# A hybrid encoder layer on one core: loads of the reverse attention a step ahead, operand splits inside the last steps of an epoch, the first row tile of the output projection between the last norms

## The chip, the core and the metric

The kernel runs on one NeuronCore of a Trainium2 chip. The metric is the device time of one execution in microseconds (us). Before the change three runs took 3528.44, 3544.09 and 3544.74 us, median 3544.09. The profiled execution took 3531.64 us and its span is 3529.9 us.

## The reference

One layer of a bidirectional encoder for 2048 tokens of width 1024, all in float32: two mixers side by side (a RWKV-7 recurrence and a gated linear attention, GLA, each run forward and backward over the sequence), an output projection, a gated FFN and a gate over per-layer embeddings.

```
xn = rms_norm(h, norm_mix_pre);  z = xn @ w_in
y_rwkv = rwkv7_mixer(z_rwkv)     # S = S*w + (S@-kk) b + v k, forward and reverse; group norm; gate
y_gla  = gla_mixer(z_gla)        # chunks of 64, forward and reverse, summed; rms_norm * silu(g)
h = h + rms_norm(concat(y_rwkv, y_gla) @ w_out, norm_mix_post)
hn = rms_norm(h, norm_ffn_pre)
f  = (silu(hn @ ffn_gate) * (hn @ ffn_up)) @ ffn_down
h = h + rms_norm(f, norm_ffn_post)
gate = sigmoid(h @ ple_gate + ple_gate_b)
h = h + rms_norm(gate * (p @ ple_proj), norm_ple)
```

## The kernel before

Three phases follow one another. The input phase (to about 1030 us) makes the projections and the forward half of GLA. The recurrence, `phase_b`, handles RWKV in 8 units of 16 steps; each step is a handful of short matmuls, and the loop also pops two lists of side work: `fill`, the reverse half of GLA (`gla_tail`: 17 items, popped on the odd steps under 12 of a unit, which the trace has between 1140 and 1391 us), and `todo`, the group norms and gates of the RWKV output, one per step. The last norms have no steps left to lie beside: they are popped in a loop of their own once the steps are done, at about 1770 to 1796 us. A norm sums and squares on VectorE (DVE) and ScalarE (ACT), takes a power on GpSimd (POOL), writes and reads the scratch `d_yn`, and is turned by TensorE (PE) into the bank `pty` before DVE multiplies it with the gate and it is stored to `d_y`.

`phase_c` begins when these are stored. It takes 16 row tiles of the output projection (`out_tile`, t = 0 to 15). A float32 product is made of three passes in fp32r: both operands are split into a high part (a cast on ACT, line 1056) and the rest (a subtraction on DVE, line 1057), and `mm3` (lines 73 to 75) adds high x high, low x high and high x low. A tile is 8 slices x 2 column halves x 3 = 48 matmuls of 128x512. Then come six epochs E0 to E5 of steps: FFN gate and up for each half of the tokens (E0, E1: 22 steps each), the FFN's down product in three parts (E2 to E4: 8 steps each) and the embedding gate (E5: 8 steps). A step multiplies by a scheme of seven products in place of eight, in the order B11, T2, B21, T3, T1, T4, B22, each of 3n matmuls (n is 3 in E2, 4 elsewhere). The moving operand of the seven products is fixed for an epoch and stays in SBUF, split; `moving` loads and splits the seven at each change of epoch, after the last step's products in the program. Each operand of n=4 is two loads (`rawm`), two casts and two subtractions of 128x1024.

All loads and stores are issued by SyncE (SP), in order. Every engine runs its instructions in one fixed order; a scheduler has set that order beforehand by the times of a simulated run, so program text that moves can change the order on all five engines. PSUM banks of the products: `pA` (pool psA), `pB`, `pC`, two each; `pt` is for transposes and for the scratch `jk` of the row norms.

Of the kernel before, what the change touches and what calls it, by code (L numbers as in the profile page):

```python
# [631 lines left out]
def phase_b(ctx, ctr, tc, k):  # L632
# [316 lines left out]
    for n in range(len(steps) + LAG):  # L949
# [35 lines left out]
    while todo:  # L985
        todo.pop(0)()


def gla_tail(k, yp, ip, ps):
# [6 lines left out]
    def step(q, h):  # L996
# [6 lines left out]
        nc.sync.dma_start(sg, k.d["sg"][128 * h:128 * h + 128, q * TQ:q * TQ + TQ])  # L1003
        po = ps.tile([128, 4, 128], F32, tag="psg", name="po")
# [27 lines left out]
    lag = []  # L1032

    def run(q, h):
        if q is not None:
            lag.append(step(q, h))
# [4 lines left out]
    return [(lambda a: lambda: run(*a))(a) for a in seq]  # L1041
# [22 lines left out]
def out_weights(ctx, tc, k):  # L1064
# [12 lines left out]
    return wo  # L1077

# [7 lines left out]
def phase_c(ctx, tc, k, wo):  # L1086
# [36 lines left out]
    def moving(e, src, r0, n, ops=OPS):  # L1123

        for o in ops:
            pool = w if o in OPS[:4] else sl
            mv[o] = []
            for b in range(0, n, 2):
                m = min(2, n - b)
                raw = cp.tile([128, 2, 512], F32, tag="t", name="rawm")[:, :m]  # L1130
                if o[0] == "B":
                    r, c = r0 + n * (o[1] == "2") + b, 512 * (o[2] == "2")
                    nc.sync.dma_start(raw, src[r:r + m, :, c:c + 512].rearrange("j p f -> p j f"))
                else:
                    nc.sync.dma_start(raw, k.d["mt"][e, int(o[1]) - 1, :, b:b + m])
                hl = [pool.tile([128, 2, 512], F32R, tag=f"{o}{b // 2}{t}", bufs=1, name=f"{o}{t}")[:, :m] for t in "hl"]
                split_into(nc, *hl, raw)
                mv[o].append(hl)
# [41 lines left out]
    def products(st, n, t):  # L1180

        def prod(bank, p, o, first):
            sh, s_l = st[p]
            if first and k.bias and bank is not B:
                k.bias(bank, int(bank is C))
                first = False
            for j in range(n):
                mm3(nc, bank, sh[:, j], s_l[:, j], mv[o][j // 2][0][:, j % 2], mv[o][j // 2][1][:, j % 2], first and j == 0, j == n - 1, skip_group_check=True)
# [5 lines left out]
        prod(A, 1, "B11", True)  # L1194
        p1 = u("p1")
# [3 lines left out]
        V.tensor_add(u2, B, p1)  # L1199
        prod(A, 2, "B21", False)  # L1200
        prod(B, 7, "T3", False)
        u3 = u("u3")
        V.tensor_add(u3, B, p1)
        while late and late[0][0] <= t:
            late.pop(0)[1]()
        prod(C, 5, "T1", True)
        c = [cp.tile([128, D], F32, tag="t", name="c") for _ in range(2)]
        V.tensor_add(c[1][:, 512:], C, u3)
        prod(B, 4, "T4", False)
        V.tensor_add(c[1][:, :512], B, p1)  # L1210
        prod(C, 3, "B22", False)
# [50 lines left out]
    def out_split(raw, m):  # L1262
        hl = []
        for g in range(2):
            hl.append([sp.tile([128, 4, 128], F32R, tag="s" + x, name="s" + x) for x in "hl"])
            split_into(nc, *hl[g], raw[:, 4 * g:4 * g + 4, 128 - 128 * m:256 - 128 * m])
        return hl

    def out_tile(t, i, hl):
        x = xtile(rows("x", i))  # L1270
        A = psA.tile([128, 512], F32, tag="pA", name="pA")
        B = psB.tile([128, 512], F32, tag="pB", name="pB")
        for c, bank in enumerate((A, B)):
            for j in range(KT):
                mm3(nc, bank, *[v[:, j % 4] for v in hl[j // 4]], *[v[:, j % 2] for v in wo[c][j]], j == 0, j == KT - 1)
            if c == 0:
                while late and late[0][0] <= t:
                    late.pop(0)[1]()
        r = root([A, B])
# [9 lines left out]
        late.append((t + 2, lambda: transposed(x, k.d["hT"][p // 4, :, :, q:q + 128].rearrange("k p t -> p k t"), True)))  # L1289

    def out_projection():
        raws = [out_operand(0), out_operand(1)]
        hl = out_split(raws[0], 0)
        e = E[0]
        for t in range(16):
            p, m = t // 2, t % 2
            nx = out_split(raws[(t + 1) // 2], 1 - m) if t < 15 else prepare(0)
            out_tile(t, PAIRS[p][m], hl)
# [5 lines left out]
            if t == 14:  # L1304
                flush()
                moving(0, e.src, e.r0, e.n, OPS[4:])
            hl = nx
        moving(0, e.src, e.r0, e.n, OPS[:4])
# [68 lines left out]
    def pre_ple(c_):  # L1377
        return [xtile(rows("e", PAIRS[c_][m])) for m in range(2)]

    def post_ple(c_, x, A, c):  # L1380
        S.activation(c[0][:, :512], A, AF.Sigmoid)
        res = [xtile(rows("h2", PAIRS[c_][m])) for m in range(2)] if c_ == 7 else x
# [55 lines left out]
    for t, (e, i) in enumerate(steps):  # L1438
# [10 lines left out]
        A, c = products(st, ep.n, 16 + t)  # L1449
# [4 lines left out]
        if i + 1 == len(ep.parts) and e + 1 < len(E):  # L1454
            nxt = E[e + 1]
            moving(e + 1, nxt.src, nxt.r0, nxt.n)
# [78 lines left out]
def body(tc, k):  # L1535
    with ExitStack() as ctx:
# [23 lines left out]
        next(b, None)  # L1560
# [18 lines left out]
```

## Time and profile before

| | before |
|---|---|
| runs, us | 3528.44, 3544.09, 3544.74 (median 3544.09) |
| profiled execution / span, us | 3531.64 / 3529.9 |
| TensorE busy | 3322.2 us (94%) |
| VectorE / ScalarE / GpSimd busy | 2607.5 (74%) / 1705.3 (48%) / 450.5 us (13%) |
| mean granted TensorE clock | 0.962 |
| HBM moved | 403.18 MB read, 211.81 MB written |

TensorE is busy nearly all the time, so what can be gained is in two places: the gaps in which it waits, and the stretches in which its granted clock is at the lower of its two levels and the same matmul takes up to twice as long. A row of a window view gives, for each engine, the busy us and instructions in a stretch, then PEclk (the mean granted clock, 1.00 is full) and the share of DMA time. A row of a timeline gives the start, the length, the engine, the line, what is written from what, and in brackets the idle time before it and what ended it.

### The profile page before, as it was taken

The numbers are of one execution on the slowest core, as the hardware profiler recorded it, in microseconds if no ns is written. First come the engines' busy times: TensorE is split into PE (matmuls) and PEld (weight loads), VectorE is DVE, ScalarE is ACT, GpSimd is POOL, SyncE is SP. The second block draws the span as 40 slices with busy tenths as digits, with TensorE's granted clock in tenths as the row PEclk, the third lists the DMA queues.
The fourth block names the chain that finished last, engine by engine and source line by source line (L and its number), as shares of the span: only waits on it lengthen the run. The fifth ranks groups of instructions, "written<-read, shape, count | busy, mean of one in ns | idle before, by whom it ended". The sixth has DMA issues, their size and how long they took to land.

```text
span 3529.9 us, 57042 instructions
## 1 busy us (share of the span) xinstructions
PE 3322.2 (94%) x20880; PEld 2839.5 (80%) x20880; DVE 2607.5 (74%) x4481; ACT 1705.3 (48%) x3547; POOL 450.5 (13%) x898
## 2 busy tenths in 40 slices
PE   7989999989998999999879899999999999999998
PEld 6979988878976888888758688887888878778776
DVE  6998898887895667678644667777666566778887
ACT  5665566655555546665624532334332333334454
POOL 2000000000002445556111100000000000001112
PEclk9999999989998879999989999999999999999999
DMA  7766655646664445463355845556222243666775
GB/s 249 248 237 195 188 198 193 213 138 219 202 199 148 132 134 161 112 182 87 114 177 188 289 143 179 191 192 225 84 86 82 84 134 132 227 203 245 278 258 185
DMA packets 390436, 629.25 MB, mean 178 GB/s; under 512 B 122790, under 2 KB 223142, under 8 KB 390156
## 3 DMA queue, kind: packets, MB, share of 16 engines
q1 hardware_dynamic: 390156, 625.61, 53.6%
q8 instruction: 165, 2.70, 0.3%
q14 instruction: 115, 0.94, 0.1%
HBM read 403.18 MB, written 211.81 MB: 174 GB/s over the span
## 4 chain that ended last, share of the span: by engine, by line
PE 73%; DVE 12%; DMA 7%; ACT 4%; issue 3%; SPq 1%; POOL 0%; DVEq 0%; ACTq 0%; POOLq 0%
PE pB L73 7%; PE pB L75 6%; PE pB L74 6%; PE pA L74 5%; PE pA L75 5%; PE pA L73 5%; PE pC L74 4%; PE pC L75 4%; PE pC L73 4%; PE pz L73 3%; PE pz L75 3%; PE pz L74 3%; PE pg L673 3%; PE ph L792 3%; PE pf L809 2%
## 5 line engine op out<-in xcount | busy, mean ns | idle before, releaser
L1056 ACT CAST sh<-raws 128x512 fp32r<-128x512 f32 (+1 forms) x456 | 277.6, 610 | 672.8 <-PE pB L74 357.4
L73 PE MATMUL pz<-xh,wh 128*128 128x256 f32 (+1 forms) x1728 | 501.0, 291 | 13.3 <-DMA wh<-d_ws 7.1
L75 PE MATMUL pz<-xh,wl 128*128 128x258 f32 (+1 forms) x1728 | 495.9, 290 | 5.6 <-DVE wl L218 3.1
L74 PE MATMUL pz<-xl,wh 128*128 128x256 f32 (+1 forms) x1728 | 496.5, 288 | 0.2 <-DVE xl L271 0.2
L1057 DVE TENSOR_TENSOR sl<-raws,sh 128x512 fp32r<-128x512 f32 (+1 forms) x456 | 306.0, 672 | 115.8 <-ACT sh L1056 110.6
L73 PEld LDWEIGHTS pz<-xh,wh 128*128 128x128 f32 x1728 | 330.9, 192 | 22.6 <-issue 13.7
L75 PEld LDWEIGHTS pz<-xh,wl 128*128 128x128 f32 x1728 | 328.2, 191 | 15.9 <-issue 6.8
L74 PEld LDWEIGHTS pz<-xl,wh 128*128 128x128 f32 x1728 | 331.5, 192 | 6.3 <-issue 5.3
L1221 POOL TENSOR_TENSOR st<-st 128x1 f32<-128x1 f32 x64 | 17.4, 271 | 1630.4 <-ACT jk L1220 1629.9
L792 PE MATMUL ph<-x,wpi 128*128 128x128 f32 x1024 | 174.6, 300 | 11.4 <-ACT wpi L788 10.0
L73 PE MATMUL pA<-B11h,sh 128*128 128x512 f32 x360 | 147.9, 412 | 22.1 <-ACT B11h L1056 18.5
L809 PE MATMUL pf<-sv,Ht 128*128 128x64 f32 x1024 | 156.7, 283 | 10.2 <-ACT sv L814 5.8
L792 PEld LDWEIGHTS ph<-x,wpi 128*128 128x128 f32 x1024 | 142.3, 203 | 22.1 <-ACT wpi L788 16.2
L809 PEld LDWEIGHTS pf<-sv,Ht 128*128 128x128 f32 x1024 | 140.3, 201 | 22.5 <-ACT sv L814 9.4
L74 PE MATMUL pA<-B11l,sh 128*128 128x512 f32 x360 | 148.1, 411 | 4.1 <-DVE B11l L1057 4.1
L75 PE MATMUL pA<-B11h,sl 128*128 128x512 f32 x360 | 146.9, 408 | 0.0
L673 PE MATMUL pg<-ar,bk 64*128 64x128 f32 x1024 | 141.1, 295 | 5.0 <-DVE x L676 3.2
L73 PE MATMUL pB<-T3h,sh 128*128 128x512 f32 x360 | 143.4, 398 | 0.0
L75 PE MATMUL pB<-T3h,sl 128*128 128x512 f32 x360 | 143.0, 397 | 0.0
L74 PE MATMUL pB<-T3l,sh 128*128 128x512 f32 x360 | 142.5, 396 | 0.0
L1056 ACT CAST sh<-s 128x512 fp32r<-128x512 f32 (+1 forms) x76 | 46.3, 609 | 186.6 <-PE pA L74 164.0
L673 PEld LDWEIGHTS pg<-ar,bk 64*128 64x128 f32 x1024 | 119.4, 196 | 19.5 <-DVE x L676 4.2
(637 smaller groups left out, 8983.4 us busy)
## 6 DMA issues: line engine op xcount, KB each, us to landing
wh<-d_ws SPq DMA_DIRECT2D x81, 512.0 KB, 3.8
wl<-d_ws SPq DMA_DIRECT2D x81, 512.0 KB, 5.0
d_mt<-rawt SPq DMA_DIRECT2D x92, 256.0 KB, 2.5
raws<-in_ffn_gate SPq DMA_DIRECT2D x44, 512.0 KB, 4.9
raws<-in_ffn_up SPq DMA_DIRECT2D x44, 512.0 KB, 4.1
rawm<-d_mt SPq DMA_DIRECT2D x44, 512.0 KB, 8.7
d_hid<-c SPq DMA_DIRECT2D x88, 256.0 KB, 2.8
d_ar<-st SPq DMA_DIRECT2D x32, 512.0 KB, 3.7
```

The source lines that it names most:

```text
L73: nc.tensor.matmul(out, ah, bh, start=start, stop=False, **kw)
L74: nc.tensor.matmul(out, ah, bl, start=False, stop=False, **kw)
L75: nc.tensor.matmul(out, al, bh, start=False, stop=stop, **kw)
L673: nc.tensor.matmul(pg[h][:, j], bk[HR[h], j], ar[HR[h], j], start=True, stop=True)
L792: nc.tensor.matmul(ph[:, h, j], w[:, h, j], x[:, j0 + j, 4 * h:4 * h + 2, :], start=True, stop=True)
L809: nc.tensor.matmul(pf[:, h, j0 + j], H[:, h, j], SV[p, d, c][:, h, j0 + j], start=True, stop=True)
L1056: nc.scalar.copy(hi, src)
L1057: nc.vector.tensor_sub(lo, src, hi.bitcast(F32))
L1221: G.tensor_add(st[:, 2:3], st[:, 0:1], st[:, 1:2])
```

## The change

1. `gla_tail`: the loads of an item (`fetch`) are an item of their own, before the item that computes (`step`). The list is 34 long and popped on every step under 12; while it lasts, `todo` is popped on odd steps only.
2. `phase_b` yields before and after each of the norms that are left at its end. Between two of them `body` loads the 128 tokens of the first row tile of the output projection (512 KB), splits them, and runs that tile's two x 24 matmuls into two `pA` banks. Tiles from t = 1 on use the banks in another order.
3. The transposes of the last two row tiles are put off by a step.
4. `moving` is a generator. In the last step of an epoch (and in tile 15) it is resumed before the products and after the first six of them: each time one operand is loaded and the one before is split; what is left follows after the products.
5. In the last step of E5 the residual tiles are loaded before the products.

```diff
-            if s % 2 == 1 and s < 12 and fill:
+            if s < 12 and fill:
                 fill.pop(0)()
-            if todo:
+            if todo and (s % 2 or s >= 12 or not fill):
                 todo.pop(0)()
...
+    yield
     while todo:
         todo.pop(0)()
+        yield
...
+        return qi, o, sg
+
+    def step(q, h, qi, o, sg):
         po = ps.tile([128, 4, 128], F32, tag="psg", name="po")
...
+    def ahead(q, h):
+        if q is not None:
+            ready.append(fetch(q, h))
...
+    return [(lambda f, a: lambda: f(*a))(f, a) for a in seq for f in (ahead, run)]
...
+def out_products(k, hl, bank, wo):
+    for j in range(KT):
+        mm3(k.nc, bank, *[v[:, j % 4] for v in hl[j // 4]], *[v[:, j % 2] for v in wo[j]], j == 0, j == KT - 1)
...
+    def settle(o, raws):
+
+        pool = w if o in OPS[:4] else sl
+        mv[o] = []
+        for b, raw in enumerate(raws):
+            hl = [pool.tile([128, 2, 512], F32R, tag=f"{o}{b}{t}", bufs=1, name=f"{o}{t}")[:, :raw.shape[1]] for t in "hl"]
+            split_into(nc, *hl, raw)
+            mv[o].append(hl)
+
+    def moving(e, ops):
+
+        fetched = []
         for o in ops:
...
+            fetched.append((o, fetch(e, o)))
+            yield
+            if len(fetched) > 1:
+                settle(*fetched.pop(0))
+        while fetched:
+            yield
+            settle(*fetched.pop(0))
...
-    def products(st, n, t):
+    def products(st, n, t, change):
...
         prod(A, 1, "B11", True)
+        next(change, None)
         p1 = u("p1")
...
-        late.append((t + 2, lambda: transposed(x, k.d["hT"][p // 4, :, :, q:q + 128].rearrange("k p t -> p k t"), True)))
+        late.append((t + 2 + (t > 13), lambda: transposed(x, k.d["hT"][p // 4, :, :, q:q + 128].rearrange("k p t -> p k t"), True)))
...
-        A, c = products(st, ep.n, 16 + t)
+        last = i + 1 == len(ep.parts) and e + 1 < len(E)
+        change = moving(e + 1, OPS) if last else iter(())
+        next(change, None)
+        A, c = products(st, ep.n, 16 + t, change)
...
-        next(b, None)
+        next(b)
+        with ExitStack() as ef:
...
+            hl = out_split(k, fp, raw)
+            banks = [k.psA.tile([128, 512], F32, tag="pA", name="pA") for _ in range(2)]
+            for c in range(2):
+                out_products(k, hl, banks[c], mv[c])
+                next(b, None)
+        k.first = banks
+        for _ in b:
+            pass
         bl.close()
         phase_c(ctx, tc, k, mv)
```

How the order of instructions moves, at the three places that matter most. TensorE at the end of the recurrence, before; `pf` and `ph` are of the last steps, `pty` are the turned group norms, `B11h` is the first slice of the output weights and `sh` of a row tile:

```order
L869 MATMUL pty<-ident,yn 128x128 x4
L809 MATMUL pf<-sv,Ht 128x64 x4
L869 MATMUL pty<-ident,yn 128x128 x4
L809 MATMUL pf<-sv,Ht 128x64 x2
L869 MATMUL pty<-ident,yn 128x128 x16
L73 MATMUL pA<-B11h,sh 128x512
L74 MATMUL pA<-B11l,sh 128x512
L73 MATMUL pB<-B21h,sh 128x512
```

The same place after the change; the 48 matmuls into `pA` lie between the last `pf` and the last sixteen `pty`, of which the first and last ones are shown:

```order
L809 MATMUL pf<-sv,Ht 128x64 x2
L869 MATMUL pty<-ident,yn 128x128 x4
L809 MATMUL pf<-sv,Ht 128x64 x2
L73 MATMUL pA<-B11h,sh 128x512
L74 MATMUL pA<-B11l,sh 128x512
...
L74 MATMUL pA<-T3l,sh 128x512
L75 MATMUL pA<-T3h,sl 128x512
L869 MATMUL pty<-ident,yn 128x128 x16
L73 MATMUL pB<-B11h,sh 128x512
L74 MATMUL pB<-B11l,sh 128x512
```

Before, the sixteen `pty` of the last two norms stood in front of the first row tile; now they stand behind all of it and in front of the second.

VectorE at the change from E0 to E1, before; `c<-pC` and `c<-pB` empty the last step's banks, `sl` and `raws` belong to the next step's stationary operand, `B11l` and `T2l` are the next epoch's splits:

```order
L1203 TENSOR_TENSOR u_25790<-pB,p_25750 128x512
L1115 TENSOR_TENSOR rawt<-rawt 128x512
L1057 TENSOR_TENSOR sl<-s_25698,sh 128x512
L1208 TENSOR_TENSOR c<-pC,u_25790 128x512
...
L1210 TENSOR_TENSOR c<-pB,p_25750 128x512
...
L1212 TENSOR_TENSOR c<-pC,u_25764 128x512
...
L1057 TENSOR_TENSOR B11l<-rawm,B11h 128x1024 x2
L1057 TENSOR_TENSOR T2l<-rawm,T2h 128x1024 x2
```

The same place after the change:

```order
L1247 TENSOR_TENSOR u_25828<-pB,p_25764 128x512
L1137 TENSOR_TENSOR rawt<-rawt 128x512
L1066 TENSOR_TENSOR sl<-s_25704,sh 128x512
L1066 TENSOR_TENSOR B11l<-rawm,B11h 128x1024
...
L1066 TENSOR_TENSOR B11l<-rawm,B11h 128x1024
L1066 TENSOR_TENSOR T2l<-rawm,T2h 128x1024
...
L1066 TENSOR_TENSOR T2l<-rawm,T2h 128x1024
L1066 TENSOR_TENSOR B21l<-rawm,B21h 128x1024
...
L1253 TENSOR_TENSOR c<-pC,u_25828 128x512
L1256 TENSOR_TENSOR c<-pB,p_25764 128x512
```

Five splits of 128x1024 now stand ahead of the two instructions that empty `pC` and `pB`; they stood behind them.

SyncE at the same change, before; `rawt` are loads for later operands, `rawm` the next epoch's own:

```order
L1147 DMA raws<-in_ffn_up 128x1024 x2
L1112 DMA rawt<-in_ple_gate 128x1024 x2
L1120 DMA d_mt<-rawt 128x512 x3
L1327 DMA d_hid<-c 128x4x128
L1120 DMA d_mt<-rawt 128x512
L1133 DMA rawm<-d_hT 128x2x512 x2
```

The same place after the change:

```order
L1187 DMA raws<-in_ffn_up 128x1024 x2
L1134 DMA rawt<-in_ple_gate 128x1024 x2
L1153 DMA rawm<-d_hT 128x2x512 x2
L1155 DMA rawm<-d_mt 128x1024 x2
L1153 DMA rawm<-d_hT 128x2x512
L1142 DMA d_mt<-rawt 128x512 x3
```

The first two `rawm` loads no longer stand behind the stores of `rawt` and of the step's result.

## Rows read from the trace of the kernel before

**Rows 1.** The page's chain that ended last, by engine.

```profile
PE 73%; DVE 12%; DMA 7%; ACT 4%; issue 3%; SPq 1%; POOL 0%; DVEq 0%; ACTq 0%; POOLq 0%
```

**Rows 2.** Waits of TensorE, whole span: us in total, times, longest.

```profile
PE pA L73 <- ACT B11h L1056: 18.5, 5, 6.0
PE pty L869 <- DVE yn L851: 13.7, 2, 8.1
...
PE po L1014 <- DMA qi<-d_qb: 9.8, 5, 3.7
PE pt L1238 <- ACT jk L1220: 9.7, 2, 8.7
```

**Rows 3.** Windows of 250 us of the recurrence, with and without the GLA items.

```profile
1150.00:1400.00 250.00, 234.83 (x1999) 210.29 (x1998) 175.46 (x379) 137.12 (x441) 123.31 (x213) 0.85 0.50 141
1400.00:1650.00 250.00, 241.82 (x2809) 222.25 (x2809) 178.71 (x391) 152.97 (x430) 138.78 (x270) 1.00 0.50 137
```

**Rows 4.** Timeline of TensorE: three of its waits in the GLA stretch.

```profile
1181.35 0.46 PE L1014 MATMUL po<-sbt,qi 64*128 64x128 f32 x2 [1.77 <-DMA qi<-d_qb]
...
1229.55 0.41 PE L780 MATMUL pt<-ident,x 128*128 128x128 f32 x2 [0.94 <-DMA x<-d_ar]
...
1282.12 0.46 PE L1014 MATMUL po<-sbt,qi 64*128 64x128 f32 x2 [1.67 <-DMA qi<-d_qb]
```

**Rows 5.** Windows of the GLA stretch that begin at waits of TensorE.

```profile
1142.00:1162.00 20.00, 19.27 (x106) 17.76 (x107) 11.11 (x27) 7.77 (x26) 1.02 (x1) 0.66 0.22 65
1181.00:1197.00 16.00, 15.65 (x81) 13.52 (x82) 8.74 (x20) 7.91 (x27) 8.79 (x12) 0.68 0.50 136
...
1230.00:1265.00 35.00, 35.00 (x258) 29.92 (x257) 14.82 (x29) 14.65 (x48) 6.35 (x14) 0.51 0.44 119
1282.00:1290.00 8.00, 7.88 (x60) 7.19 (x60) 6.37 (x13) 4.43 (x16) 5.89 (x8) 1.00 0.45 133
1304.00:1319.00 15.00, 14.35 (x63) 12.91 (x64) 12.60 (x25) 4.15 (x14) 6.12 (x13) 0.56 0.33 100
```

**Rows 6.** Timeline of TensorE from the last steps into row tile 1.

```profile
1777.47 1.09 PE L869 MATMUL pty<-ident,yn 128*128 128x128 f32 x4 [8.08 <-DVE yn L851]
...
1795.91 0.80 PE L73 MATMUL pA<-B11h,sh 128*128 128x512 f32 x1 [3.10 <-ACT sh L1056]
...
1799.49 0.63 PE L73 MATMUL pA<-B11h,sh 128*128 128x512 f32 x1
1799.92 0.63 PE L74 MATMUL pA<-B11l,sh 128*128 128x512 f32 x1
...
1800.76 0.39 PE L73 MATMUL pA<-B11h,sh 128*128 128x512 f32 x1
...
1809.42 0.39 PE L73 MATMUL pA<-B11h,sh 128*128 128x512 f32 x1
```

**Rows 7.** Timelines of SyncE and of ScalarE there: the row tile's load and split.

```profile
1789.27 1.16 SPq L1259 DMA_DIRECT2D rawy<-d_y  x2
...
1795.24 2.18 ACT L1056 CAST sh<-rawy 128x512 fp32r<-128x512 f32 x4 [12.46 <-DMA rawy<-d_y]
```

**Rows 8.** Timeline of TensorE: waits at four changes of epoch.

```profile
2008.18 1.97 PE L1238 MATMUL pt<-ident,x 128*128 128x128 f32 x8 [8.71 <-ACT jk L1220]
...
2443.79 0.80 PE L73 MATMUL pA<-B11h,sh 128*128 128x512 f32 x1 [5.39 <-ACT B11h L1056]
...
2881.85 0.80 PE L73 MATMUL pA<-B11h,sh 128*128 128x512 f32 x1 [6.02 <-ACT B11h L1056]
...
3168.63 0.51 PE L73 MATMUL pA<-B11h,sh 128*128 128x512 f32 x1 [1.47 <-ACT B11h L1056]
```

**Rows 9.** Timeline of SyncE in the last step of E0.

```profile
2421.27 0.90 SPq L1112 DMA_DIRECT2D rawt<-in_ple_gate  x2
...
2436.02 1.08 SPq L1133 DMA_DIRECT2D rawm<-d_hT  x2
```

**Rows 10.** Timeline of VectorE there: splits of 128x1024.

```profile
2443.77 2.56 DVE L1057 TENSOR_TENSOR B11l<-rawm,B11h 128x1024 fp32r<-128x1024 f32 x2 [2.81 <-ACT B11h L1056]
```

More of the change, by code (lines that the diff above doesn't have):

```diff
@@ L994, in gla_tail, with fetch @@
     state = [None] * 4
-    def step(q, h):
+    def fetch(q, h):
         qi = yp.tile([128, 2, 512], F32, tag="yn", name="qi")
@@ L1077, in out_weights, with out_split @@
     return wo
+def out_split(k, pool, raw):
+    hl = []
+    for g in range(2):
+        hl.append([pool.tile([128, 4, 128], F32R, tag="s" + x, name="s" + x) for x in "hl"])
+        split_into(k.nc, *hl[g], raw[:, 4 * g:4 * g + 4])
+    return hl
+def out_products(k, hl, bank, wo):
+    for j in range(KT):
+        mm3(k.nc, bank, *[v[:, j % 4] for v in hl[j // 4]], *[v[:, j % 2] for v in wo[j]], j == 0, j == KT - 1)
 def broadcast(k, pool, n, **kw):
@@ L1121, in sums, with fetch @@
         return keep
-    def moving(e, src, r0, n, ops=OPS):
-        for o in ops:
[L1126 to L1138, printed above, removed]
+    def fetch(e, o):
+        src, r0, n = E[e].src, E[e].r0, E[e].n
+        raws = []
+        for b in range(0, n, 2):
+            m = min(2, n - b)
+            raw = cp.tile([128, 2, 512], F32, tag="t", name="rawm")[:, :m]
+            if o[0] == "B":
+                r, c = r0 + n * (o[1] == "2") + b, 512 * (o[2] == "2")
+                nc.sync.dma_start(raw, src[r:r + m, :, c:c + 512].rearrange("j p f -> p j f"))
+            else:
+                nc.sync.dma_start(raw, k.d["mt"][e, int(o[1]) - 1, :, b:b + m])
+            raws.append(raw)
+        return raws
+    def settle(o, raws):
[7 more added lines that the diff above has]
+        fetched = []
+        for o in ops:
+            fetched.append((o, fetch(e, o)))
[5 more added lines that the diff above has]
+            settle(*fetched.pop(0))
     w = k.mvr
@@ L1199, in products @@
         V.tensor_add(u2, B, p1)
+        next(change, None)
         prod(A, 2, "B21", False)
+        next(change, None)
         prod(B, 7, "T3", False)
@@ L1205, in products @@
             late.pop(0)[1]()
+        next(change, None)
         prod(C, 5, "T1", True)
@@ L1208, in products @@
         V.tensor_add(c[1][:, 512:], C, u3)
+        next(change, None)
         prod(B, 4, "T4", False)
         V.tensor_add(c[1][:, :512], B, p1)
+        next(change, None)
         prod(C, 3, "B22", False)
@@ L1278, in out_tile @@
                     late.pop(0)[1]()
+                next(change, None)
+                next(change, None)
         r = root([A, B])
@@ L1305, in out_projection @@
                 flush()
[L1306 removed]
+                for _ in moving(0, OPS[4:]):
+                    pass
             hl = nx
[L1308 removed]
+        for _ in change:
+            pass
         return nx
@@ L1453, in phase_c @@
             after(sums(n, E[n].src, E[n].r0, E[n].n, j))
-        if i + 1 == len(ep.parts) and e + 1 < len(E):
-            nxt = E[e + 1]
-            moving(e + 1, nxt.src, nxt.r0, nxt.n)
+        for _ in change:
+            pass
         st = nx
@@ L1559, in body @@
         mv = out_weights(ctx, tc, k)
-        next(b, None)
+        next(b)
+        with ExitStack() as ef:
+            fp = ef.enter_context(tc.tile_pool(name="first", bufs=2, side="right", reuse_waits="tile"))
+            raw = fp.tile([128, KT, 128], F32, tag="raw", bufs=1, name="rawy")
+            q = 128 * PAIRS[0][0]
+            tc.nc.sync.dma_start(raw, k.d["y"][:, :, q:q + 128].rearrange("k p t -> p k t"))
+            hl = out_split(k, fp, raw)
[5 more added lines that the diff above has]
+        for _ in b:
+            pass
         bl.close()
```

38 lines of the change are left out of this document (18 added, 20 removed).

## The prediction

> **What bounds the kernel now.** I read the chain that ended last first [rows 1]: TensorE carries 73% of it, VectorE 12%, DMA 7%. So a change pays only where TensorE waits or runs slowly. Next come TensorE's waits [rows 2]. Four of their groups touch the diff: 18.5 us in five waits for B11h, the first split of a new epoch; 13.7 us for the normed tile `yn` at the end of the recurrence; 9.8 us in five waits for `qi`, the load of a GLA item; 9.7 us for `jk`, nearly all of it one wait of 8.7. Last I read windows for the clock. The 250 us with GLA items run at a granted 0.85, the 250 us behind them at 1.00 [rows 3]; their TensorE is 235 and 242 us busy, so the first stretch hides (1 - 0.85) x 250 = 37 us in slow matmuls, not in gaps.
>
> **GLA loads a step ahead.** The waits for `qi` are the part that the diff addresses: 9.8 us. With the loads out a step earlier (17 items at 6 to a unit of 16 steps are some 45 steps, in the 251 us from 1140 to 1391 some 5.6 us each, an estimate) a wait remains only where SyncE itself is late. I take 8 us. Behind such a wait the clock often stays low: the windows that begin at 1142, 1181 and 1304 us lose 20 x 0.34 = 6.8, 16 x 0.32 = 5.1 and 15 x 0.44 = 6.6 us, together 18.5 [rows 5]. But the link is loose: a wait of 1.67 us for the same load at 1282 is followed by a window at 1.00, and one of 0.94 us at 1229, for another load, `x`, is followed by 35 us at 0.51 that cost 17.2 [rows 4, 5]. The diff does not remove that one. I take a third of the 18.5, 6 us; the bounds are 0 (other waits drop the clock in their place) and all 37. Term: 14 us, from 0 to 46. The Trainium skill (TensorE: Matmul & The Clock Gate, HAM oscillation) has it that a wait for a DMA between bursts of matmuls sets the clock back, and that each such wait is paid for anew. By that, all of the 18.5 would go and the term would be 28; the trace agrees at three of the four places named here and not at 1282 us.
>
> The compute items themselves are unchanged, 16 of them and one that only finishes, over the same 34 steps. `todo` is popped half as often in these steps and I price that at nothing, because few norms are due so early; if they are, they move behind 1400 us, where VectorE is 179 of 250 us busy [rows 3].
>
> **Row tile 0 among the last norms.** Before, TensorE does next to nothing from 1770 to 1796, and tile 0 then takes 1809.42 - 1795.91 = 13.5 us [rows 6]: eleven matmuls at 0.43 us, the lower clock, the other 37 at (1809.42 - 1800.76) / 37 = 0.234. If all that went into the gap the gain were 13.5. But in the new order the last sixteen `pty`, those of two norms, stand behind all 48. The first of them ran at 1777.47 [rows 6]. The new load of 512 KB needs features of an earlier norm only and stands, in SyncE's order, behind loads of the last steps; I put its issue at 1765, an estimate. From issue to the first cast the load before took 1795.24 - 1789.27 = 6.0 us [rows 7], so the cast starts near 1771, the matmuls at 1771.5, and they end 12 to 13.5 us later: 1783.5 to 1785. The `pty` are then 6 to 7.5 us late, and everything behind them, 1795.91 - 1777.47 = 18.4 us of norm, stores, load and split until the next row tile starts, moves with them: 1802 to 1803.5. VectorE also gets tile 0's two splits and its norm in this stretch, up to 3 us. So tile 1 starts at 1802 to 1806.5, against 1809.42. I take 1806, as VectorE's idle time here covers some of its 3 us: a gain of about 3, from -3 (the load goes out 6 us later than I think) to 9 (early load). The price of the moved `pty` is thus some 10 of the 13.5 us.
>
> The Trainium skill (DMA: Bandwidth & Descriptors, Anatomy of one DMA) gives a transfer about 2 us plus its bytes at 436 GB/s. For 512 KB that is an estimate of 3.2 us and would put tile 0, and this term's gain, nearly 3 us better; the row has 6.0 for a load of twice the bytes, which the rule puts at 4.4, so here it is short and I stay with the row.
>
> **Splits inside the last steps.** At a change of epoch TensorE waits for B11h and then runs some ten matmuls at half pace; eleven of them at 0.43 instead of 0.234 cost 2.1 us [rows 6]. So the change E0 to E1 costs 5.39 + 2.1 = 7.5, E1 to E2 6.02 + 2.1 = 8.1, E3 to E4 1.47 + 2.1 = 3.6 [rows 8]. Of the 18.5 us of B11h waits [rows 2] 5.6 are left for E2 to E3 and E4 to E5: nearly all for E2 to E3, 7.5 with its slow matmuls. From the projection to E0 the wait of 8.71 for `jk` [rows 8] and slow matmuls make 11.
>
> What is gained of each:
> - The loads move up. Before, the first `rawm` goes out at 2436.02, and in the new order it follows the `rawt` loads that start at 2421.27 [rows 9]; B11's splits started at 2443.77 [rows 10], 7.7 us behind the issue, so they can now start at about 2430, ahead of the end of the step's products.
> - The work doesn't vanish. A pair of splits takes VectorE 2.56 us [rows 10], seven pairs 18 us per change, in a step whose TensorE work is 84 x 0.234 = 19.7 us. VectorE is 74% of the span busy as it is, so 0.74 x 19.7 + 18 = 32.5 us of its work meet one step, and two steps have 39.4 for 47. Part of the stall therefore returns as a wait on VectorE. The order shows where: five splits now stand ahead of the copies that empty `pC` and `pB`, 5 x 1.28 = 6.4 us, and the last product needs `pC`. TensorE has two or three products of 2.8 us to do meanwhile, so about 2 us of new wait at that change.
>
> E0 to E1: 7.5 - 2 = 5.5. E1 to E2: its loads come from an input and stand right behind the step's own, I take 7 of 8.1. E2 to E3: its first loads stay behind a store of the step, I take 4.5 of 7.5. E3 to E4: 3 of 3.6. Projection to E0: B11 is now split after the row norm on ScalarE; I take 3.5 of 11. E4 to E5 had waits of many kinds and still has its first loads behind a store: 2, from -3 to 5. Sum 25.5. The lower end supposes that VectorE returns two thirds of it (8), the upper one that all but the projection's goes (35).
>
> The two late transposes move between products that don't wait for them, and the earlier residual loads of E5 hide under products: nothing for both.
>
> **Sum.** 14 + 3 + 25.5 = 42.5 us off 3531.64, the profiled execution's own time: 3489. That execution lies 12.5 us under the median of the runs, 3544.09; against the median the forecast is 3544.1 - 42.5, about 3502.
>
> **Rivals.**
> 1. VectorE takes the stalls back. For: 32.5 us of work in a step of 19.7. Against: between changes VectorE has slack on both sides. The changes then give 8, the GLA loads only the waits, 8, the row tile 3: 19 off, 3525.
> 2. The clock comes back in the whole GLA stretch. For: the stretch behind it, the same steps without the items, runs at 1.00 [rows 3]. Against: the longest slow window follows another load [rows 4, 5]. Then 46 + 3 + 25.5 = 74 off, 3470.
> 3. Slower: the new loads get in the way of the steps' own. SyncE is in order, and each `fetch` now puts four loads, the first of them waiting for the one `yn` buffer, ahead of the `x` loads of the running step. Price: the wait of 0.94 us for `x` at 1229 led into a window that cost 17.2 us [rows 4, 5]. Two such new falls, 34 us, eat the 28.5 of the rest, with no gain from the GLA loads; from the third the kernel is slower by over 0.5%: 28.5 - 51.6 = 23 us, 3567. For: SyncE's queue is where TensorE's waits there come from. Against: the sixteen compute items need the same loads either way.
> 4. The edits don't take effect, because the scheduler had hoisted the loads where it could: 3544 less 0 to 10. Against it stand SyncE's rows before and after, where the first loads move ahead of the stores.
>
> **Chances.** Forecast (3485 to 3518) 0.58; rival 1 0.17; rival 2 0.13; rival 3 0.06; rival 4 0.06. About 0.5%, 17.7 us, is what a measurement of this kernel can tell from no change: faster means under 3526.4. The forecast, rival 2 and half of rival 1 with some more make 0.80; the rest of rival 1 and most of rival 4 make 0.14 for no change; slower 0.06. The range reaches from rival 2 to the far side of rival 1: 3467 to 3533.
>
> **What would show it.** In the new profile: the `qi` waits under 2 us in all and the clock of 1150 to 1400 us at 0.88 or more; 48 matmuls between 1765 and 1790, the last sixteen `pty` after them, tile 1 30 to 35 us after the first of the 48 rather than 13.5; B11h waits under 6 us in all, with new waits for `c` at the last product of a last step. It is wrong if the stretch before 1770 grows, if tile 1 starts later against the last `pf` than before, or if waits for `c` come to more than 15 us.

## The result

The changed kernel takes 0.9946 of the time of the one before (95% interval 0.9928 to 0.9963): median 3528.03 us against 3544.41, 19 us less by the ratio. A second comparison gave 0.9942 (0.9918 to 0.9966). The forecast was 42 us less, 3502. The sign was right, and the forecast gain is more than twice the measured one. The first ratio leaves out one execution of each kernel that took far longer, 8696.96 and 5060.71 us.

The page of the changed kernel, its span and the chain that ended last, answers to [rows 1]:

```profile
span 3526.9 us, 57066 instructions
...
PE 73%; DVE 13%; DMA 6%; ACT 4%; issue 3%; SPq 0%; POOL 0%; DVEq 0%; POOLq 0%; ACTq 0%
```

TensorE's waits over its whole span, beside [rows 2] (us in total, times, longest):

```profile
PE pA L73 <- ACT B11h L1065: 13.8, 5, 5.5
...
PE pty L869 <- DVE yn L851: 8.8, 1, 8.8
...
PE pC L73 <- DVE c L1253: 5.7, 3, 4.5
PE pB L73 <- ACT sh L1065: 5.7, 1, 5.7
...
PE po L1019 <- DMA qi<-d_qb: 4.9, 3, 2.3
...
PE po L1019 <- DMA qi<-d_ib: 3.7, 1, 3.7
```

The waits for B11h fell only from 18.5 to 13.8, where the forecast had under 6. Two groups are new (`pC` for `c`, `pB` for `sh`). For `qi` the two groups together are 8.6, against 9.8 before and a forecast of under 2. The windows of [rows 3] after the change, with a granted clock of 0.87 in the first, where 0.88 or more was forecast:

```profile
1150.00:1400.00 250.00, 232.87 (x2035) 210.67 (x2035) 180.39 (x386) 139.34 (x448) 129.39 (x223) 0.87 0.51 144
1400.00:1650.00 250.00, 243.09 (x2742) 223.17 (x2740) 173.88 (x383) 150.92 (x422) 134.14 (x260) 0.99 0.49 134
```

One profile against one says little here: these two spans differ by 3 us, the medians by 16. So I dated the same places in every profile and compared the stretches between them. In the recurrence, step k begins with the VectorE instruction that writes `Ht` for the k-th time, counted from 0. A step of an epoch (numbered 0 to 75 through all epochs) is dated by the add that empties `pC` behind T1. The last inverse is the last of the recurrence's small 32x32 matmuls. For the last stretch, from step 58 to step 71, these are the rows of VectorE before the change

```profile
3146.88 0.68 DVE L1208 TENSOR_TENSOR c<-pC,u 128x512 f32<-128x512 f32 x1
...
3438.57 0.69 DVE L1208 TENSOR_TENSOR c<-pC,u 128x512 f32<-128x512 f32 x1
```

and after it

```profile
3135.55 0.68 DVE L1253 TENSOR_TENSOR c<-pC,u 128x512 f32<-128x512 f32 x1
...
3435.41 0.68 DVE L1253 TENSOR_TENSOR c<-pC,u 128x512 f32<-128x512 f32 x1
```

that is 291.7 and 299.9 us. The same for all stretches and for the kernels of the experiments below (us):

| kernel | recurrence, steps 0-112 | last inverse to step 3 of E0 | E0 to E1 (19-27) | E1 to E2 (41-46) | E2 to E3 (50-54) | E3 to E5 (58-71) |
|---|---|---|---|---|---|---|
| before | 572.2 | 377.9 | 165.2 | 93.6 | 81.3 | 291.7 |
| before, second profile | 588.9 | 379.5 | 164.6 | 94.1 | 81.6 | 288.1 |
| GLA part alone | 566.1 | 381.6 | 165.2 | 95.7 | 82.0 | 289.6 |
| epochs' part alone | 578.1 | 378.4 | 160.0 | 86.6 | 78.2 | 301.6 |
| changed | 571.8 | 379.6 | 160.0 | 87.1 | 79.0 | 299.9 |
| changed, second profile | 558.1 | 376.2 | 160.1 | 87.1 | 79.2 | 300.6 |
| changed, no early row tile | 572.3 | 378.9 | 160.0 | 86.6 | 79.0 | 301.3 |
| changed, E5 loaded late | 567.4 | 378.8 | 160.0 | 87.8 | 77.1 | 290.9 |
| changed, few resumptions | 568.6 | 375.9 | 160.0 | 87.1 | 76.9 | 290.1 |

Between kernels with the same part for the epochs, the last four stretches repeat to 1 to 4 us; the recurrence does not. The last stretch got 11 us longer wherever the epochs' part stands as in the change.

### The profile page after: what moved, and what is told of

Same layout as the page of the kernel before. It is cut to its first block, busy times and chain, and to the rows that moved or that the text cites. A ratio compares the mean times of both kernels' runs of the same rounds, so it can differ in the third digit from the quotient of the medians.

```text
span 3526.9 us, 57066 instructions
## 1 busy us (share of the span) xinstructions
PE 3323.2 (94%) x20880; PEld 2841.6 (81%) x20880; DVE 2603.8 (74%) x4481; ACT 1708.6 (48%) x3547; POOL 449.8 (13%) x898
## 4 chain that ended last, share of the span: by engine, by line
PE 73%; DVE 13%; DMA 6%; ACT 4%; issue 3%; SPq 0%; POOL 0%; DVEq 0%; POOLq 0%; ACTq 0%
PE pB L73 6%; PE pB L75 6%; PE pB L74 6%; PE pA L74 5%; PE pA L73 5%; PE pA L75 5%; PE pC L74 4%; PE pC L75 4%; PE pC L73 4%; PE pz L73 3%; PE pz L75 3%; PE pz L74 3%; PE pg L673 3%; PE ph L792 3%; PE pf L809 3%
## 5 line engine op out<-in xcount | busy, mean ns | idle before, releaser
L809 PEld LDWEIGHTS pf<-sv,Ht 128*128 128x128 f32 x1024 | 142.4, 204 | 21.3 <-DVE Ht L794 6.3
L74 PE MATMUL pA<-B21l,sh 128*128 128x512 f32 x360 | 143.5, 399 | 0.0
L74 PE MATMUL pB<-T2l,sh 128*128 128x512 f32 x356 | 141.9, 399 | 1.5 <-DVE T2l L1066 1.4
L75 PE MATMUL pA<-B21h,sl 128*128 128x512 f32 x360 | 143.0, 397 | 0.0
L73 PE MATMUL pA<-B21h,sh 128*128 128x512 f32 x360 | 142.9, 397 | 0.0
L75 PE MATMUL pB<-T2h,sl 128*128 128x512 f32 x356 | 141.9, 399 | 0.0
L73 PE MATMUL pB<-T2h,sh 128*128 128x512 f32 x356 | 141.8, 398 | 0.1
L788 ACT COPY wpi<-pt 64x256 f32<-64x256 f32 x256 | 93.9, 367 | 98.9 <-PE pt L784 94.4
L73 PE MATMUL pA<-B11h,sh 128*128 128x512 f32 x300 | 123.1, 411 | 18.3 <-ACT B11h L1065 13.8
```

Of the source, the lines that this page charges most:

```text
L73: nc.tensor.matmul(out, ah, bh, start=start, stop=False, **kw)
L74: nc.tensor.matmul(out, ah, bl, start=False, stop=False, **kw)
L75: nc.tensor.matmul(out, al, bh, start=False, stop=stop, **kw)
L788: S.copy(w[HR[h], h], pt[HR[h], 2:4])
L809: nc.tensor.matmul(pf[:, h, j0 + j], H[:, h, j], SV[p, d, c][:, h, j0 + j], start=True, stop=True)
```

## The experiments

**E5 loaded late.** In the last step of E4 nothing is resumed; all of E5's operands follow the products.

```diff
-        next(change, None)
-        A, c = products(st, ep.n, 16 + t, change)
+        now = change if e + 2 < len(E) else iter(())
+        next(now, None)
+        A, c = products(st, ep.n, 16 + t, now)
```

> The changed kernel, but the operands of E5 are loaded and split behind the last products of E4, as before the change; all other parts stay. Theory A (the loads of E5 wait for buffers of the pool that the last step of E4 still holds, and the splits that wait for them stand in VectorE's order ahead of the copies that empty the banks): between the steps before and after this change of epoch the kernel wins back the 8.5 us that the changed kernel loses there against the one before, and the whole run is 8.5 us faster than the changed kernel, a ratio of about 0.992 against the kernel before. Rival B (VectorE simply has too much to do there wherever the splits stand): the 8.5 us stay, ratio 0.9946.

Ratio 0.9941 (0.9923 to 0.9958). The stretch from step 58 to step 71 takes 290.9: the loss is gone from its place, as theory A has it. By its time alone this kernel can't be told from the changed one (0.9946).

**No early row tile.**

```diff
...
-        hl = None
+        hl = out_split(k, sp, raws[0][:, :, 128:256])
...
-            out_tile(t, PAIRS[p][m], hl, change, None if t else k.first)
+            out_tile(t, PAIRS[p][m], hl, change, None)
...
-            for c in range(2):
-                out_products(k, hl, banks[c], mv[c])
-                next(b, None)
-        k.first = banks
```

> The changed kernel with row tile 0 back in the output projection, behind all norms. Theory A (the 48 matmuls delay the last sixteen pty by as much as they save): tile 1 starts 2 us earlier or later than in the changed kernel, counted from the last matmul of the recurrence's small inverses, ratio 0.994 to 0.995. Rival B (tile 0 is worth the 3 us of the forecast): tile 1 starts 3 to 5 us later than in the changed kernel, ratio 0.9955.

Ratio 0.9972 (0.9948 to 0.9996), above both expectations. Tile 1 starts 104.0 us behind the last inverse, against 102.1 and 98.5 in the two profiles of the changed kernel; the stretch from the last inverse to step 3 of E0 takes 378.9, against 379.6 and 376.2. So few profiles decide nothing. Over all profiles of this study the six without the early tile have a mean of 379.4 in that stretch (377.9 to 381.6), the twelve with it 376.1 (373.1 to 379.6), and tile 1 starts at 102.5 and 98.1. The tile is worth 3 to 4 us by these means, rival B; the kernels of the two groups differ in other parts too.

**The GLA part alone**, on the kernel before (part 1 of the change):

> The kernel before with the GLA loads a step ahead, and nothing else of the change. Theory A (GLA makes most of the gain): 12 to 15 us faster, ratio 0.996, the waits for qi fall from 9.8 us to 5 or less and the stretch of the GLA items gets shorter by 6 us or more. Rival B (the gain comes from the changes of epoch): ratio 0.999, within 4 us of the kernel before.

Ratio 0.9976 (0.9952 to 1.0), 8.5 us, between the two. The waits for `qi` hardly fell, from 9.8 to 8.9 us:

```profile
PE po L1017 <- DMA qi<-d_qb: 8.9, 5, 3.5
```

**The epochs' part alone** (parts 3 to 5 of the change):

> The kernel before with the splits inside the last steps of the epochs, the later transposes and the earlier residual loads, without the GLA and the row tile parts. Theory A (5 to 6 us at each of two changes of epoch, 2 at a third, nearly nothing at two, and 8.5 lost at the last): 6 us faster, ratio 0.998. Rival B (these parts carry the whole gain): 17 to 20 us faster, ratio 0.995.

Ratio 0.9988 (0.997 to 1.0006): theory A. Its gains of 5 us (E0 to E1) and 7 us (E1 to E2) are eaten by the last changes of epoch.

**Few resumptions.** In the last step of E4 `change` is resumed ahead of the products, behind the add that follows T1 and behind the one that follows T4, and not in between; `few` is true in that step alone.

```diff
+        later, change = change, iter(()) if few else change
         next(change, None)
...
         V.tensor_add(c[1][:, 512:], C, u3)
-        next(change, None)
+        next(later, None)
         prod(B, 4, "T4", False)
         V.tensor_add(c[1][:, :512], B, p1)
-        next(change, None)
+        next(later, None)
```

> The changed kernel, but in the last step of E4 the next epoch's operands are handled only at three places: the first load ahead of the products, then one load and one split each behind the copies that follow T1 and T4; the rest behind the products. Theory A (the loss comes from splits that wait for late loads and stand ahead of the copies that empty pC and pB): no wait of TensorE for c over 1.5 us in that step, and the change from E4 to E5 costs no more than in the kernel before (290 us from step 58 to step 71 of the epochs, against 300 in the changed kernel), perhaps 3 less. Rival B (VectorE has too much to do): 297 us or more.

Ratio 0.992 (0.9893 to 0.9947), the stretch from 58 to 71 takes 290.1. All of TensorE's waits from 3300 to 3340 us:

```profile
PE pA L73 <- ACT B11h L1065: 2.8, 2, 1.6
PE pA L74 <- DVE B11l L1066: 1.2, 2, 0.8
PE pt L1286 <- ACT x L1293: 0.2, 1, 0.2
PE pB L73 <- DVE u L1248: 0.2, 1, 0.2
```

No wait for `c` is left. VectorE has the same splits to do, so rival B falls. The loads that are still early give nothing here: the stretch takes as long when all is loaded late (290.9).

**Ten buffers** in the pool shared by loads, results and residual tiles; to make room, the pool of the split row operands has one less.

```diff
-    sp = pool("stat", 7)
+    sp = pool("stat", 6)
...
-    cp = pool("cc", 9)
+    cp = pool("cc", 10)
```

> The changed kernel with ten buffers in place of nine in the pool that the operands' loads, the results and the residual tiles share (and six in place of seven in the pool of split row operands, to make room). If the loads of E5 are late because they wait for a buffer (SyncE waits for T2l, B21l, T3l and T1l there), one more buffer lets each go out one operand-half earlier and the stretch from step 58 to step 71 falls from 300 to 296 or less. If the DMA engines themselves are the limit (0.87 to 1.03 busy there), it stays at 299 to 301.

The stretch takes 293.2 in this one profile, 7 us less than with nine buffers. The add of step 63 parts the two changes of epoch in it. From 63 to 71, where E4 to E5 lies, it takes 185.1, against a mean of 195.1 with nine buffers and of 184.6 without the epochs' part: the loss of that change is gone, although a wait of 4.47 us for `c` is left. From 58 to 63 it takes 108.0, against 105.4. Other places lost as well: E1 to E2 takes 93.1, against 87.1, and from step 71 to the end 96.3, against 91.5.

**The inverse that is formed during unit 3 a step later**, on the kernel with E5 loaded late.

```diff
-            if nu and s == (7 if u.i else 8):
+            if nu and s == (7 if u.i not in (0, 3) else 8):
```

> The kernel with the old change to E5 (the experiment that undid it), and one more edit in the recurrence: the second stage of the inverse that is formed during unit 3 comes a step later (at step 8 of the unit in place of 7), which puts 12 rows of other matmuls ahead of its 32x32 matmuls on TensorE. Theory C (the GLA stretch gains some 12 us, and 17 of them are given back behind it, because the new order makes TensorE wait 2.0 us for the transposed tile un just ahead of a run of 32x32 matmuls, and the granted clock falls to 0.50 for some 25 us): the wait is gone or under 1 us, steps 56 to 64 of the recurrence take 36 us as in the kernel before and not 53, and the whole is 15 us faster than the same kernel without the edit, ratio 0.990 against the kernel before. Rival D (the clock falls there for another reason, such as the time since the GLA items ended): steps 56 to 64 take 44 to 56 us again, ratio 0.994.

Ratio 0.9905 (0.9877 to 0.9933), steps 56 to 64 took 41.2. That fits theory C, but the two kernels run beside it, without the edit, took 40.5 there. So it is not shown. The fall itself is seen in the kernel with E5 loaded late, in a row of TensorE and a window:

```profile
1464.28 1.20 PE L722 MATMUL pq<-un,x 32*32 32x32 f32 x64 [2.03 <-DVE un L714]
```

```profile
1464.00:1494.00 30.00, 29.72 (x300) 26.80 (x301) 11.37 (x31) 11.11 (x29) 2.73 (x8) 0.54 0.32 83
```

TensorE is busy 29.7 of 30 us there, at 0.54; steps 56 to 64 took 52.7 us. The same wait of 2.0 us with such a fall behind it stands in three other kernels (GLA part alone, with one buffer and with two; no early row tile). But the kernel with few resumptions has that wait and no fall, and the kernel below with the projection's change undone has the edit, no wait ahead of these matmuls, and a longer fall; its steps 56 to 64 took 56.4 us. First a row and a window of the former, then a window of the latter:

```profile
1475.87 1.20 PE L722 MATMUL pq<-un,x 32*32 32x32 f32 x64 [2.08 <-DVE un L714]
```

```profile
1475.00:1505.00 30.00, 28.67 (x389) 26.11 (x389) 22.54 (x55) 17.81 (x47) 7.20 (x15) 1.00 0.55 148
```

```profile
1468.00:1506.00 38.00, 37.05 (x330) 33.65 (x331) 15.71 (x40) 15.13 (x42) 4.75 (x12) 0.52 0.39 114
```

So that wait is neither enough for a fall nor needed for one, and theory C does not hold as it was put.

**Two buffers for `qi`** on the changed kernel.

```diff
-                Y[p, gi] = yp.tile([128, 8, 64], F32, tag="y", bufs=6, name="y")
+                Y[p, gi] = yp.tile([128, 8, 64], F32, tag="y", bufs=5, name="y")
...
-        yn = yp.tile([128, 8, 2, 64], F32, tag="yn", bufs=1, name="yn")
+        yn = yp.tile([128, 8, 2, 64], F32, tag="yn", bufs=2, name="yn")
...
-        qi = yp.tile([128, 2, 512], F32, tag="yn", name="qi")
+        qi = yp.tile([128, 2, 512], F32, tag="yn", bufs=2, name="qi")
```

> The changed kernel with two buffers in place of one for the tiles qi and yn, and five in place of six for the sums y to make room. Theory E (the loads of qi are called a step earlier, but SyncE holds each back until the item before has used the one buffer, 21.7 us of waits for sbt and po, so they land as late as before): the waits of TensorE for qi fall from 8.6 us to under 3, apart from the first one of 3.7, and the first 48 steps of the recurrence take 285 us or less, against 295 in the changed kernel and 277 to 285 in three others with the same GLA part. Rival F (something else than the buffer holds the loads): the waits stay at 8 us or more.

Ratio 0.9907 (0.9886 to 0.9928). The one wait for `qi` in 1140 to 1400 us that is left in the view is the first one:

```profile
PE po L1019 <- DMA qi<-d_ib: 2.8, 1, 2.8
```

Theory E for the waits. Steps 0 to 48 take 284 us, as expected, but that shows nothing: the second profile of the changed kernel, with one buffer, took 285 there.

**Both edits that were tried one by one** (few resumptions, the inverse a step later).

> The changed kernel with the few resumptions in the last step of E4 and with the second stage of unit 3's inverse a step later: the two edits that were tried one by one, together. If they add up: a ratio of 0.989 against the kernel before, some 20 us faster than the changed kernel. If the inverse's edit does nothing (steps 56 to 64 took 40.5 us in two kernels without it): 0.992.

Ratio 0.9886 (0.986 to 0.9912), as if the two added up; the interval overlaps that of few resumptions alone, so what the inverse's edit gives is not shown.

**The kernel before, second profile.**

> The kernel before once more, for a second profile of it: the profiled execution shown ahead of the prediction lies 12.5 us under the median of its runs. If that one had a lucky clock in the recurrence, steps 0 to 64 take some 375 us here and not 367, and the epochs from step 3 on the same 1351 us as before. If the epochs differ, the landmarks of one profile can't be compared with those of another.

Its time was 3552.21 us. Steps 0 to 64 took 372.6 us, and steps 72 to 80 53.1 against 42.7 in the first profile, at a granted 0.77 there (1.00 in the first). The epochs from step 3 to step 71 took 1347.9, against 1351.3. So the profile that the forecast was made from had a lucky recurrence; its granted clock over steps 0 to 112 was the highest of the three profiles without the GLA part.

**All three edits**, and **the same with the projection's change to E0 undone**:

```diff
-        late.append((t + 2 + (t > 13), ...
+        late.append((t + 2, ...
...
-            next(change, None)
-            out_tile(t, PAIRS[p][m], hl, change, None if t else k.first)
+            out_tile(t, PAIRS[p][m], hl, none, None if t else k.first)
```

> The three edits that did something, together, on the changed kernel: two buffers for qi (and five for y), the few resumptions in the last step of E4, the inverse of unit 3 a step later. The edits lie in different stretches. If their gains add up: 10 us of the recurrence by the buffer, 10 at the change from E4 to E5, so some 20 to 25 us faster than the changed kernel's 0.9946, a ratio of 0.987 to 0.988 against the kernel before. If the buffer and the inverse's edit were the same gain seen twice: 0.990 or more.

> The kernel just named, but the first operands of E0 are loaded and split behind row tile 15 and the late transposes are not put off, both as in the kernel before. If this part of the change gave the 3.5 us of the forecast: from the last small inverse to step 3 of E0 takes 3 us or more longer than in the kernel with it, ratio 0.001 higher. If a wait of 5.5 us for B11h only took the place of the wait of 8.7 us for jk: the same within 2 us.

The ratios are 0.9944 (0.9917 to 0.997) and 0.9967 (0.9943 to 0.999). The gains did not add up. For the projection the stretch behind the last inverse decides: 375.6 without its change, 373.4 and 377.3 with it in the two profiles of all three edits: no gain to be seen. The profiled execution of all three edits took 3535.31 us, where the median is 3513.41, and shows where the time went: 592.9 us for steps 0 to 112. Two of its windows:

```profile
1140.00:1240.00 100.00, 90.06 (x674) 82.42 (x673) 62.62 (x134) 48.08 (x157) 42.42 (x78) 0.78 0.43 128
...
1559.00:1606.00 47.00, 44.57 (x481) 41.17 (x480) 24.10 (x52) 25.18 (x71) 24.23 (x50) 0.85 0.53 147
```

**Four kernels once more on one chip**, to settle the GLA term: the changed one; the GLA part with two buffers, alone on the kernel before; all three edits; the same without the buffer.

> The changed kernel once more. If the change from E4 to E5 is what the trace showed, steps 58 to 71 take 300 us again, and the epochs before it the same to 1 us; steps 0 to 112 of the recurrence may lie anywhere from 560 to 590 us. Ratio 0.9945 against the kernel before.

> The kernel before with the GLA loads a step ahead, two buffers for qi and yn and five for y, and nothing else of the change. Theory E (the single buffer kept the loads from going out early): waits for qi under 3 us, and the kernel is 15 us or more faster than the one before, ratio 0.9955 or less. Rival G (what the waits gave is taken back by falls of the clock at other places): the waits fall, the ratio stays at 0.997 to 0.999.

> The changed kernel with all three edits (two qi buffers, few resumptions in the last step of E4, the inverse of unit 3 a step later), once more, beside the kernel without the buffer. Theory E: 8 us or more faster than that kernel. Rival G: the same or slower.

> The changed kernel with the few resumptions and the inverse's edit only, once more, on the same chip as the kernel with the buffer. Ratio 0.988 to 0.990 against the kernel before if the earlier call can be repeated.

In this order the ratios are 0.9942 (0.9918 to 0.9966), 0.996 (0.9937 to 0.9983), 0.9938 (0.9912 to 0.9964) and 0.9893 (0.9857 to 0.9928). The GLA part with two buffers waits 3.0 us for `qi`:

```profile
PE po L1017 <- DMA qi<-d_qb: 3.0, 1, 3.0
```

It is 14 us faster than the kernel before; the same part with one buffer was 8.5 faster, and the intervals overlap. Beside the other two edits the buffer costs some 16 us, on the same chip; the other two edits alone came out at 0.9886 and 0.9893, the best version of the study, some 38 us under the kernel before. Why the buffer hurts there stays open: the profiled execution of that kernel (562.1 us for steps 0 to 112) took 3509.58 us, 12 under its median, and does not show it.

## Why the prediction failed, step by step

The step that failed is the change from E4 to E5, "2, from -3 to 5", and beside it E3 to E4, "3 of 3.6". The two share a stretch, and it lost 11.0 (mean of four profiles without the epochs' part, 289.4; of five with it as in the change and nine buffers, 300.4). That is 16 of the 21 us by which the forecast missed the sum below. The add of step 63 parts them: by the same means E4 to E5 (63 to 71) went from 184.6 to 195.1, a loss of 10.5, and E3 to E4 (58 to 63) from 104.8 to 105.4. E3 to E4 gained nothing: in the two profiles compared here its wait for B11h fell from 1.5 to 0.2 us, but all waits of TensorE from 58 to 63 went from 3.4 to 3.7, with new ones for T1l, T2l and `c`.

Of E4 to E5 I had seen that the loads stay behind a store, and that splits stand ahead of the copies that empty `pC`, and I priced the second at 2 us for E0 to E1 alone. Here both meet, and the prediction's own term had no price for it. TensorE in the changed kernel:

```profile
3329.63 0.79 PE L73 MATMUL pA<-B11h,sh 128*128 128x512 f32 x1 [4.30 <-ACT B11h L1065]
...
3345.96 0.80 PE L73 MATMUL pC<-B22h,sh 128*128 128x512 f32 x1 [4.55 <-DVE c L1253]
...
3361.83 0.50 PE L1421 MATMUL pC<-mvb,one 128*128 128x512 f32 x1 [2.94 <-DVE c L1259]
```

VectorE just ahead of the second of them:

```profile
3343.96 1.23 DVE L1066 TENSOR_TENSOR T3l<-rawm,T3h 128x1024 fp32r<-128x1024 f32 x1 [2.22 <-ACT T3h L1065]
3345.22 0.69 DVE L1253 TENSOR_TENSOR c<-pC,u 128x512 f32<-128x512 f32 x1
```

VectorE was idle 2.2 us for a split whose operand was not there, with the copy that TensorE waited for queued behind it. Before the change that copy ran 9 us earlier, although step 58 came 11 us later:

```profile
3336.43 0.69 DVE L1208 TENSOR_TENSOR c<-pC,u 128x512 f32<-128x512 f32 x1
```

And SyncE was late for two reasons, by its waits from 3318 to 3360 us. A load stands behind the store of a turned tile `x` and needs its buffer (5.3 and 3.1 us), and the loads need buffers that earlier splits free (11.0 us together):

```profile
SPq L1293 <- ACT x L1292: 5.3, 1, 5.3
SPq L1155 <- DVE T3l L1066: 3.5, 1, 3.5
SPq L1155 <- DMA d_h2T<-x: 3.1, 1, 3.1
SPq L1153 <- DVE T4l L1066: 3.1, 1, 3.1
SPq L1153 <- DVE B11l L1066: 2.3, 1, 2.3
SPq L1153 <- DVE T1l L1066: 2.1, 1, 2.1
```

A ring: load, split, buffer, next load, and TensorE's bank in the middle of it. Taking the splits out of the copies' way (few resumptions) took the loss away with the same work on VectorE. One buffer more took it away too, in one profile and with the wait of 4.47 us for `c` still there. So the ring is shown at both of its ends; how much of the 10.5 us the order makes and how much the buffers is not separated.

The other changes of epoch came near the forecast, by the same four and five profiles: E0 to E1 5.0 (5.5 forecast), E1 to E2 7.4 (7), E2 to E3 3.1 (4.5). At E0 to E1 about 2 us of new waits had been forecast; 1.5 stood where the order had put them:

```profile
2443.53 0.50 PE L74 MATMUL pB<-T2l,sh 128*128 128x512 f32 x1 [0.64 <-DVE T2l L1066]
...
2445.87 0.50 PE L73 MATMUL pC<-B22h,sh 128*128 128x512 f32 x1 [0.90 <-DVE c L1253]
```

The projection to E0, "3.5 of 11", gave nothing that the stretches show: the wait of 8.71 for `jk` [rows 8] became one of 5.5 for B11h, beside the 3.9 for T1h that was 3.1 before.

```profile
2010.79 0.80 PE L73 MATMUL pA<-B11h,sh 128*128 128x512 f32 x1 [5.52 <-ACT B11h L1065]
```

Row tile 0 gave some 3 us of the 13.5 by the means above, as forecast, and the price stood where the forecast had it: the last sixteen `pty` begin right behind the 48, and tile 1 starts 21.6 us behind the first of them, against 18.4 before [rows 6]. TensorE in the changed kernel:

```profile
1776.55 0.80 PE L73 MATMUL pA<-B11h,sh 128*128 128x512 f32 x1 [2.24 <-ACT sh L1065]
...
1778.43 0.95 PE L809 MATMUL pf<-sv,Ht 128*128 128x64 f32 x4
...
1790.86 0.60 PE L869 MATMUL pty<-ident,yn 128*128 128x128 f32 x4
...
1802.21 1.08 PE L869 MATMUL pty<-ident,yn 128*128 128x128 f32 x4 [8.77 <-DVE yn L851]
...
1812.44 0.79 PE L73 MATMUL pB<-B11h,sh 128*128 128x512 f32 x1 [5.68 <-ACT sh L1065]
```

Tile 1 starts 35.9 us behind the first of the 48 (30 to 35 forecast). The load and its first cast:

```profile
1770.67 0.59 SPq L1614 DMA_DIRECT2D rawy<-d_y  x1
```

```profile
1775.88 1.14 ACT L1065 CAST sh<-rawy 128x512 fp32r<-128x512 f32 x2 [4.97 <-DMA rawy<-d_y]
```

From issue to cast it took 5.2 us; the row before had 6.0 for twice the bytes [rows 7]. The 3.2 us that the prediction worked out by the Trainium skill (DMA: Bandwidth & Descriptors, Anatomy of one DMA) is too short here; the section gives that rule for transfers that GpSimd issues, and this load is SyncE's. The size of the term is partly luck. The load went out 5.7 us later than the 1765 assumed, for which the prediction had -3, and in the two profiles compared here tile 1 does start later, 102.1 us behind the last inverse against 100.0; the gain is in the means alone. One price was not seen: four of the 48 stand ahead of the last `pf`, which waited with them for the tile's split.

The GLA term came near in size, 13.5 us (mean of three profiles without it 579.7 for steps 0 to 112, of ten with it and one buffer 566.2; 14 forecast), though the three lie between 572 and 589 and the comparison by time gave 8.5 with an interval from 0 to 17. Its step was wrong, so the size is luck. "A wait remains only where SyncE itself is late" assumed that the loads go out a step earlier. They could not, as SyncE's waits from 1140 to 1400 us show: the load of `qi` (line 1000) waits until the item before has used the only buffer, and the load of the gate `sg` (line 1005) waits longer still, for the store of an earlier item.

```profile
SPq L1005 <- DMA d_y<-sgl: 15.1, 8, 3.0
...
SPq L1000 <- DVE sbt L1018: 11.6, 9, 2.3
SPq L1000 <- PE po L1019: 10.1, 4, 5.2
```

I had named that buffer in the third rival and not drawn it into the term. Of the 8 us of waits 1.2 went. What the part gains is clock. (1 - granted clock) x time is what the lower clock cost in a window; here it is taken over steps 0 to 112, before (two profiles) and after (two profiles):

```profile
1136.42:1708.63 572.21, 538.29 (x5447) 488.24 (x5446) 405.39 (x908) 329.91 (x987) 288.50 (x544) 0.93 0.47 129
1141.82:1730.66 588.84, 556.09 (x5447) 505.93 (x5446) 405.73 (x908) 329.96 (x987) 291.00 (x544) 0.90 0.45 125
```

```profile
1137.78:1709.59 571.81, 538.01 (x5447) 490.09 (x5446) 405.90 (x909) 330.06 (x987) 289.92 (x544) 0.93 0.46 129
1142.04:1700.09 558.05, 526.44 (x5447) 479.37 (x5446) 405.38 (x909) 330.30 (x987) 289.26 (x544) 0.95 0.48 132
```

That cost has a mean of 50 us in the three profiles without the part and of 34 in the ten with it and one buffer; the rest of the time has means of 529 and 532 and did not fall. The gain lies at places that the new order moved: steps 8 to 16 take 46 to 48 us in all ten profiles and 58 to 59 before, steps 72 to 80 39.5 to 40.6 and 43 to 53 before, and part is given back in steps 56 to 64 (36 to 44 before, 40 to 56 after). Which wait sets which fall is not shown. The Trainium skill (TensorE: Matmul & The Clock Gate, HAM oscillation) has a wait for a DMA between bursts of matmuls set the clock back. Of the waits for a load, the 1.77 us at 1181 agree with it and the 1.67 us at 1282 do not [rows 4, 5].

Sum of what was measured: 13.5 + 3.3 (row tile and projection) + 5.0 + 7.4 + 3.1 - 11.0 = 21.3, against 19 and 21 by the two ratios. That the sum comes so near owes something to chance, as the recurrence varies by more than these terms.

Of the rivals, the first (VectorE takes the stalls back: 3525) came nearest: 3528.03 was measured. But its mechanism was not the one at work: the amount of VectorE's work was no limit, its order was.

## What to carry to other kernels

A split that waits for a load, put ahead of the instruction that empties a bank on the same engine, makes the matmuls wait for the load: bring work forward behind the copies, not ahead of them. A load that is called earlier goes out earlier only if there is a buffer for it; look for who frees it in SyncE's waits of the kernel before. Where the clock varies, compare stretches over several profiles, and take the clock's cost out before reading the rest. Price each change of epoch by its own pool and queue and not by those of another.

## What the runs showed of the hardware

Steps 0 to 112 of the recurrence took 557.6 to 592.9 us over the study's eighteen profiles, at a mean granted clock of 0.96 in the shortest and 0.89 in the longest. Without (1 - granted clock) x time 526 to 539 us are left, so most of the spread, 1% of the kernel, is clock. The falls, to 0.5, came at changing places. The epochs from step 3 to step 71 repeated to 4 us in 1350 in the four profiles without their part (1347.9 to 1352.0). A wait of 2 us ahead of the same matmuls was followed by 30 us at 0.54 in one kernel and by 30 us at 1.00 in another, and 38 us at 0.52 came in a third kernel without it.
